# Hybrid mLSTM/attention block on one core: two weight tiles split in an earlier stage, five buffers for the later modulation vectors, one gate on another engine

## The chip, the core and the metric

The kernel runs on one core of a Trainium2 chip. A core has five engines that run side by side and meet at semaphores: TensorE (PE, matrix products and transposes into PSUM), VectorE (DVE), ScalarE (ACT), GpSimd (POOL) and SyncE (SP, which here issues every DMA, in its own order). Each engine works through its instructions strictly in the order in which they stand. The metric is the device time of one execution in microseconds, the median of several runs; lower is better.

## What is computed

One layer over 1024 latent tokens and 256 context tokens, width 1024, float32. The core of it, shortened from the reference:

```python
mod_x = silu(c) @ w_ada + b_ada                       # six vectors of 1024
sh_m, sc_m, gt_m, sh_f, sc_f, gt_f = split(mod_x, 6)
px = modulate(rms_norm(x, g_pre_mix), sh_m, sc_m) @ w_in   # and pc for the context
aq, ak, av, mq, mk, mv, mo, mg = split(px)
att = window_attention(rope(aq), rope(ak), av, kc, vc, sink)
h   = mlstm_bidir(silu(conv(mq)), silu(conv(mk)), mv, mg)   # forward and backward
ml  = rms_norm(h) * gain * sigmoid(mo)
x   = x + gt_m * rms_norm(concat(att, ml) @ w_out, g_post_mix)
f   = swiglu(modulate(rms_norm(x, g_pre_ffn), sh_f, sc_f))
x   = x + gt_f * rms_norm(f, g_post_ffn)
```

## The kernel before

**Products.** Each float32 operand of the large products is split into two fp32r parts, high and low (`split`, lines 58-61: a cast on ACT writes the high part, a subtraction on DVE the low one), and a product is three matmuls: high times high, high times low, low times high.

**Stages up to the attention**, with their times in the profiled execution:

1. to about 40 us: the modulation vectors of the mixing layer (`w_ada`, sections 0 and 1), and the transposed, modulated tokens `hh`, `hl`, `ch`, `cl`.
2. about 40 to 126 us, the V stage: token tiles times the weight slabs for the values and gates (`s1`, `s2`). In its second half `gates()` works out the mLSTM gates, and `ml_weights(n)`, for the eight token blocks n, loads rows of the gates (`w<-a_d`, 512 KB per block), adds and masks them on DVE (L489, eight instructions), exponentiates on ACT (L490), and stores the block to `w_dr` (L491). The blocks n = 0 to 7 lie in the buffers 6, 7, 8, 15, 12, 6, 7, 8 of the shared pool `R`.
3. about 126 to 305 us, the transposed projections: 13 tiles of 128 columns, in the order of `TILES` (mk0, mk1, ak, mq0, mq1, aq0 to aq3, mo0 to mo3). `tload(j)` loads tile j's weights into `tw` (buffer 13 + j % 2) and splits them into `th` (9 + j % 2) and `tl` (11 + j % 2); `tproj(j)` multiplies (L545, L546 with `th`, L548 with `tl`), for the first three tiles with the context's columns (`tc`) as a third output. Then `conv` or `rope` or a sigmoid takes the result from PSUM. Tile j + 1 is loaded while tile j is multiplied.
4. Beside the projections three more sections of `w_ada` are summed on DVE: `ada_rest(sec, j)` streams eight blocks `wb` of 512 KB through two buffers and does `acc += wb * silu(c)` (L596); section 4 after tile ak, section 3 after mq1, section 2 after aq1. `ada_rest2(sec)` reduces `acc` over the partitions on PE (L612 and, for section 2, L606). State steps of the mLSTM (`pk` L643, `mkc` L645, `pu` L649) run between the tiles.

From about 305 us on come the attention with the mLSTM outputs, the output projection (from about 467 us) and the SwiGLU layer.

**What sets the order.** Up to the attention's end, the order on each engine is not that of the code: a scheduler builds it from an own model of durations, under the data's dependencies. A buffer's next user waits for the last user of the same buffer. `issue_after` keeps a DMA behind another on SP; the `wb` blocks of a section stand behind the load of a named tile.

**Transition to the attention.** The last tile, mo3, goes through a sigmoid on ACT (L723) and is scaled by the gain on DVE (L724), then stored. The first attention item's scores (PE L881), their masked copy with a running minimum (DVE L883), exponentials (ACT L892), reciprocal (DVE L894) and normalisation (POOL L897) follow.

## Time and profile before

| | us |
|---|---|
| median of three runs | 1220.74 |
| the three runs | 1224.12, 1219.05, 1220.74 |
| the profiled execution: time | 1219.35 |
| the profiled execution: first to last instruction (span) | 1217.6 |
| PE busy in the span | 1178.2 (97%) |
| DVE, ACT, POOL busy | 819.3, 573.7, 153.4 |
| granted TensorE clock | 0.998 |

The profile names an instruction by its line, engine, operation and tiles; in a row of the timeline the first two numbers are its start and its duration in us, and what stands in brackets is how long the engine had stood idle before it and what ended the idle time. In the view of the waits, a row is: engine and waiting instruction, what released it, total us, times, longest. "SPq" is SP's queue, whose instructions issue DMAs; the time to landing is counted from the issue.

### The profile page before, as it was taken

To read this page: it belongs to the slowest core of one execution; us is meant where nothing else is said; L and a number is where in the kernel's file an instruction comes from. 1 tells how busy PE (TensorE), PEld (TensorE's weight loads), DVE (VectorE), ACT (ScalarE), POOL (GpSimd) and SP (SyncE) were. 2 spreads that over 40 slices of the span, in tenths; PEclk is the share of its full clock that TensorE was granted. 3 is DMA by queue.
4 is the path that set the end of the run, shared out by engine and by line. 5 is a ranking of instruction groups with operands and counts; after the bars stand their busy time and mean duration, and the time that the engine had idled before them with its cause. 6 is when DMAs were issued, how large, how long until landed. Compare 5 with 4: busy or idle time off the path is not lost.

```text
span 1217.6 us, 16271 instructions
## 1 busy us (share of the span) xinstructions
PE 1178.2 (97%) x5859; PEld 963.1 (79%) x5859; DVE 819.3 (67%) x1437; ACT 573.7 (47%) x1066; POOL 153.4 (13%) x196
## 2 busy tenths in 40 slices
PE   6899999999999999999999999999999999999997
PEld 1699788768778777787778888888888888888886
DVE  4873767782888796457867677767867656554566
ACT  5553424121767695777633333333334325434443
POOL 1550001224433382000000000000000000000000
PEclk9999999999999999999999999999999999999999
DMA  9521964767844411421134466466644647665853
GB/s 354 178 70 42 320 201 122 220 176 194 243 128 127 147 49 35 173 89 67 59 106 165 149 217 217 187 233 211 221 154 150 213 149 260 207 217 185 305 191 122
DMA packets 100008, 208.59 MB, mean 171 GB/s; under 512 B 9684, under 2 KB 38740, under 8 KB 98520
## 3 DMA queue, kind: packets, MB, share of 16 engines
q1 hardware_dynamic: 99928, 207.56, 51.5%
q8 instruction: 46, 0.75, 0.3%
q14 instruction: 34, 0.28, 0.1%
HBM read 154.04 MB, written 52.83 MB: 170 GB/s over the span
## 4 chain that ended last, share of the span: by engine, by line
PE 83%; DVE 7%; ACT 4%; DMA 3%; issue 2%; SPq 1%; POOL 0%; DVEq 0%; ACTq 0%
PE xv L74 8%; PE xv L72 8%; PE xv L73 8%; PE pt L74 5%; PE pt L72 5%; PE pt L73 5%; PE t L546 3%; PE t L548 3%; PE t L545 3%; PE op L74 2%; PE op L73 2%; PE op L72 2%; PE fx L72 2%; PE fx L74 2%; PE fx L73 2%
## 5 line engine op out<-in xcount | busy, mean ns | idle before, releaser
L61 DVE TENSOR_TENSOR fo<-fr,fo 128x1024 fp32r<-128x1024 f32 x77 | 92.8, 1223 | 71.4 <-ACT fo L60 66.6
L60 ACT CAST fo<-fr 128x1024 fp32r<-128x1024 f32 x77 | 79.6, 1051 | 74.0 <-PE pt L74 33.2
L545 PE MATMUL t<-hh,th 128*128 128x512 f32 x208 | 82.6, 397 | 0.0
L546 PE MATMUL t<-hl,th 128*128 128x512 f32 x208 | 82.2, 395 | 0.0
L1297 ACT CAST wS<-wr 128x512 fp32r<-128x512 f32 x88 | 54.2, 622 | 55.8 <-PE pt L74 37.4
L1299 DVE TENSOR_TENSOR wS<-wr,wS 128x512 fp32r<-128x512 f32 x88 | 60.4, 689 | 20.7 <-ACT wS L1297 20.7
L548 PE MATMUL t<-hh,tl 128*128 128x512 f32 x208 | 65.4, 394 | 3.0 <-DVE tl L61 3.0
L72 PE MATMUL xv<-tT,wS 128*128 128x512 f32 x168 | 66.1, 393 | 0.0
L74 PE MATMUL xv<-tT,wS 128*128 128x512 f32 x168 | 65.7, 391 | 0.0
L73 PE MATMUL xv<-tT,wS 128*128 128x512 f32 x168 | 65.6, 390 | 0.0
L72 PE MATMUL op<-woh,mh 128*128 128x512 f32 x128 | 51.1, 399 | 1.8 <-ACT mh L60 1.8
L74 PE MATMUL op<-woh,ml 128*128 128x512 f32 x128 | 50.4, 394 | 0.9 <-DVE ml L61 0.8
L73 PE MATMUL op<-wol,mh 128*128 128x512 f32 x128 | 50.0, 391 | 0.0
L1049 DVE TENSOR_TENSOR wr<-wr 128x512 f32<-128x512 f32 x66 | 45.5, 690 | 1.4
L545 PEld LDWEIGHTS t<-hh,th 128*128 128x128 f32 x208 | 39.1, 188 | 8.4 <-issue 0.5
L548 PEld LDWEIGHTS t<-hh,tl 128*128 128x128 f32 x208 | 37.4, 188 | 10.4 <-DVE tl L61 3.2
L546 PEld LDWEIGHTS t<-hl,th 128*128 128x128 f32 x208 | 39.1, 188 | 8.0 <-issue 1.2
L1331 ACT ACTIVATE es<-es 128x512 f32<-128x512 f32 x22 | 13.9, 633 | 66.6 <-DVE es L1052 66.6
L881 PE MATMUL s<-k,qh 128*128 128x256 f32 (+1 forms) x128 | 41.0, 330 | 2.4 <-DVE sm L883 2.2
L72 PE MATMUL pt<-fo 128*128 128x512 f32 x110 | 42.9, 390 | 0.0
L74 PE MATMUL pt<-fo 128*128 128x512 f32 x110 | 42.8, 389 | 0.0
L73 PE MATMUL pt<-fo 128*128 128x512 f32 x110 | 42.8, 389 | 0.0
(993 smaller groups left out, 3401.8 us busy)
## 6 DMA issues: line engine op xcount, KB each, us to landing
wr<-in_wfi SPq DMA_DIRECT2D x44, 512.0 KB, 5.4
wb<-in_wada SPq DMA_DIRECT2D x24, 512.0 KB, 4.4
s_d<-a SPq DMA_DIRECT2D x22, 512.0 KB, 6.6
bt<-in_wfo SPq DMA_DIRECT2D x44, 256.0 KB, 3.7
tb_d<-bt SPq DMA_DIRECT2D x11, 1024.0 KB, 3.9
fr<-s_d SPq DMA_DIRECT2D x44, 256.0 KB, 4.2
fr<-tb_d SPq DMA_DIRECT2D x44, 256.0 KB, 4.4
fr<-a_d SPq DMA_DIRECT2D x33, 256.0 KB, 4.5
```

The source lines that it names most:

```text
L60: act.copy(hi, raw)
L61: dve.tensor_tensor(lo, raw, hi.bitcast(F32), SUB)
L72: pe.matmul(ps, a[0], b[0], start=first, stop=False, **kw)
L73: pe.matmul(ps, a[0], b[1], start=False, stop=False, **kw)
L74: pe.matmul(ps, a[1], b[0], start=False, stop=last, **kw)
L545: pe.matmul(o, wh[:, kt], m[0], start=f, stop=False)
L546: pe.matmul(o, wh[:, kt], m[1], start=False, stop=False)
L548: pe.matmul(o, wl[:, kt], m[0], start=False, stop=l)
L881: pe.matmul(o, qh[:, h, :], k2[g][:, kc], start=True, stop=False)
L1049: dve.tensor_tensor(out, a, b, SUB)
L1297: act.copy(w[:, 0], raw)
L1299: dve.tensor_tensor(w[:, 1], raw, w[:, 0].bitcast(F32), SUB)
```

## The change

Three parts.

1. **Tile loads.** `tload` is moved ahead of the loop of the V stage's last products; tiles 0 and 1 are loaded and split there, ahead of `ml_weights`, and the loop over `TILES` starts its loads with tile 2. Block 4 of `ml_weights` moves from buffer 12 (that of tile 1's low part) to buffer 5.
2. **Five buffers.** The blocks `wb` of `ada_rest` go through five buffers of the pool `p2` in place of two.
3. **Last gate.** For mo3 alone the scaling by the gain is done by POOL in place of DVE.

```diff
     def ml_weights(n):
 
-        wt_ = R((6, 7, 8, 15, 12)[n % 5], f"w{n}", (2, 4, P))
+        wt_ = R((6, 7, 8, 15, 5)[n % 5], f"w{n}", (2, 4, P))
...
+    twd, tws = {}, {}
+
+    def tload(j):
+        wh = R(9 + j % 2, f"th{j}", (KT, P), F32R)
+        wl = R(11 + j % 2, f"tl{j}", (KT, P), F32R)
+        with tc.issue_after(xd[NI - 1].ins):
+            twd[j] = load_split(wh, wl, wt[j], R(13 + j % 2, f"tw{j}", (KT, P)))
+        tws[j] = wh, wl
+
     gates()
     for i in range(NFILL, NI):
         s2(i)
+        if i in (NFILL + 1, NFILL + 2):
+            tload(i - NFILL - 1)
         if i > NFILL:
             ml_weights(i - NFILL - 1)
...
             for kt in range(KT):
-                t = T((1, 3)[kt % 2], f"wb{sec}_{kt}")
+                t = T((1, 3, 4, 5, 6)[kt % 5], f"wb{sec}_{kt}")
                 dma(t, wada[kt * P:(kt + 1) * P, sec * D:(sec + 1) * D])
...
-    tload(0)
     for j, name in enumerate(TILES):
-        if j + 1 < len(TILES):
+        if 1 < j + 1 < len(TILES):
             tload(j + 1)
...
-            dve.tensor_scalar(t, t, vec[:, VGML + i:VGML + 1 + i], None, MUL)
+            g_ = vec[:, VGML + i:VGML + 1 + i]
+            if i == 3:
+                pool.tensor_scalar(t, t, g_, 1.0, MUL, MUL)
+            else:
+                dve.tensor_scalar(t, t, g_, None, MUL)
             dma(so_d[i], t)
```

The scheduler's order changes with it. The rows below are instructions in the order in which they stand on one engine, without times.

DVE, from the last blocks of `ml_weights` into the convolution of tile mk0, before. `w_1281` and `w_1295` are blocks 6 and 7, `tl_1340` is the low part of tile 1, `tl_1440` that of tile 2, `ct` the convolution, `acc_1650` the sum of section 4:

```order
L489 SCALAR_TENSOR_TENSOR w_1281<-w_1281,ucol,mB 128x128 x4
L489 SCALAR_TENSOR_TENSOR w_1295<-w_1295,ucol,mF 128x128 x4
L61 TENSOR_TENSOR tl_1340<-tw_1341,th_1339 128x1024
L489 SCALAR_TENSOR_TENSOR w_1295<-w_1295,ucol,mB 128x128 x4
L61 TENSOR_TENSOR tl_1440<-tw_1441,th_1439 128x1024
L564 TENSOR_SCALAR ct<-cr,vec 128x1024
L565 SCALAR_TENSOR_TENSOR ct<-cr,vec,ct 128x1024
L566 SCALAR_TENSOR_TENSOR ct<-cr,vec,ct 128x1024
L596 SCALAR_TENSOR_TENSOR acc_1650<-wb_0_1652,csil,acc_1650 128x1024
```

The same place after the change (`w_1293` and `w_1307` are blocks 6 and 7; later lines have moved, so that L599 was L596 and L567 to L569 were L564 to L566):

```order
L489 SCALAR_TENSOR_TENSOR w_1293<-w_1293,ucol,mB 128x128 x4
L599 SCALAR_TENSOR_TENSOR acc_1650<-wb_0_1652,csil,acc_1650 128x1024
L599 SCALAR_TENSOR_TENSOR acc_1650<-wb_1_1655,csil,acc_1650 128x1024
L61 TENSOR_TENSOR tl_1440<-tw_1441,th_1439 128x1024
L567 TENSOR_SCALAR ct<-cr,vec 128x1024
L489 SCALAR_TENSOR_TENSOR w_1307<-w_1307,ucol,mF 128x128 x4
L489 SCALAR_TENSOR_TENSOR w_1307<-w_1307,ucol,mB 128x128 x4
L568 SCALAR_TENSOR_TENSOR ct<-cr,vec,ct 128x1024
L599 SCALAR_TENSOR_TENSOR acc_1650<-wb_2_1658,csil,acc_1650 128x1024
L569 SCALAR_TENSOR_TENSOR ct<-cr,vec,ct 128x1024
```

Tile 1's low part has left this place (it now stands in the V stage, behind the low part `hl_103` of token tile 7); two sums of section 4 stand ahead of tile 2's low part, and block 7 and a third sum inside the convolution.

SP, the DMA issues from the table `sint` on, before. `w_dr_944` to `w_dr_947` are the stores of blocks 4 to 7, `tw_1541` and `tw_1678` the weights of tiles 3 and 4, `wb_0` and so on the blocks of section 4:

```order
L516 DMA sint<-in_sinc 128x1024
L487 DMA w_1295<-a_d 128x512
L491 DMA w_dr_944<-w_1227 128x1024
L487 DMA w_1295<-a_d 128x512
L491 DMA w_dr_945<-w_1267 128x1024
L491 DMA w_dr_946<-w_1281 128x1024
L65 DMA tw_1541<-in_wt 128x1024
L595 DMA wb_0_1652<-in_wada 128x1024
L595 DMA wb_1_1655<-in_wada 128x1024
L491 DMA w_dr_947<-w_1295 128x1024
L65 DMA tw_1678<-in_wt 128x1024
```

The same place after the change (L528 was L516, L598 was L595):

```order
L528 DMA sint<-in_sinc 128x1024
L598 DMA wb_0_1652<-in_wada 128x1024
L598 DMA wb_1_1655<-in_wada 128x1024
L491 DMA w_dr_944<-w_1239 128x1024
L487 DMA w_1307<-a_d 128x512 x2
L598 DMA wb_2_1658<-in_wada 128x1024
L598 DMA wb_3_1661<-in_wada 128x1024
L598 DMA wb_4_1664<-in_wada 128x1024
L491 DMA w_dr_945<-w_1279 128x1024
L491 DMA w_dr_946<-w_1293 128x1024
```

Tile 3's load has left (it stands in the V stage now, ahead of `a_d`); two blocks of section 4 are issued ahead of block 7's loads and three more ahead of the stores of blocks 5 and 6.

DVE, the sums of section 2 beside the tiles aq1 to aq3, before (`mkc` is the scaled key of a state step, `tl_2214` and `tl_2368` low parts of later tiles, `cs` the state, `aq` and `rb` the rotary step):

```order
L596 SCALAR_TENSOR_TENSOR acc_2068<-wb_3_2080,csil,acc_2068 128x1024
L645 TENSOR_TENSOR mkc<-pk,wkcol 128x256 x2
L61 TENSOR_TENSOR tl_2214<-tw_2215,th_2213 128x1024
...
L596 SCALAR_TENSOR_TENSOR acc_2068<-wb_6_2089,csil,acc_2068 128x1024
L61 TENSOR_TENSOR aq_2174<-aq_2174,aqh_2184 128x1024
L596 SCALAR_TENSOR_TENSOR acc_2068<-wb_7_2092,csil,acc_2068 128x1024
L645 TENSOR_TENSOR mkc<-pk,wkcol 128x256 x2
```

The same place after the change (L599 was L596, L648 was L645, L585 was L582):

```order
L599 SCALAR_TENSOR_TENSOR acc_2068<-wb_4_2083,csil,acc_2068 128x1024
L648 TENSOR_TENSOR mkc<-pk,wkcol 128x256 x2
L61 TENSOR_TENSOR tl_2214<-tw_2215,th_2213 128x1024
...
L599 SCALAR_TENSOR_TENSOR acc_2068<-wb_7_2092,csil,acc_2068 128x1024
L585 TENSOR_TENSOR aq_2174<-aq_2174,rb 128x1024
L61 TENSOR_TENSOR aq_2174<-aq_2174,aqh_2184 128x1024
L648 TENSOR_TENSOR mkc<-pk,wkcol 128x256 x2
```

One more sum stands ahead of the first `mkc`, and the last sum stands ahead of two instructions of the rotary step that it stood behind or between.

More of the change, by code (lines that the diff above doesn't have):

```diff
@@ L521, in T @@
         return q2.tile([P, S], F32, name=name, tag=f"s{i}")
-    twd, tws = {}, {}
-    def tload(j):
-        wh = R(9 + j % 2, f"th{j}", (KT, P), F32R)
-        wl = R(11 + j % 2, f"tl{j}", (KT, P), F32R)
-        with tc.issue_after(xd[NI - 1].ins):
-            twd[j] = load_split(wh, wl, wt[j], R(13 + j % 2, f"tw{j}", (KT, P)))
-        tws[j] = wh, wl
     def tproj(j, with_ctx):
```

## The prediction

> **What bounds the kernel now.** I read the page first:
>
> ```profile
> PE 1178.2 (97%) x5859; PEld 963.1 (79%) x5859; DVE 819.3 (67%) x1437; ACT 573.7 (47%) x1066; POOL 153.4 (13%) x196
> ```
>
> PE is busy for 1178.2 of 1217.6 us. No matmul is removed, so the change can only fill PE's idle time, 39.4 us over the whole program, and only that part of it which lies where the change acts. The second view is therefore PE's waits, between 90 and 310 us, the V stage's second half to the attention's start:
>
> ```profile
> PE t L548 <- DVE tl L61: 3.0, 1, 3.0
> PE s L881 <- DVE sm L883: 1.6, 1, 1.6
> PE pu L649 <- DVE mkc L645: 1.6, 1, 1.6
> PE ar L606 <- PE t L548: 1.0, 1, 1.0
> PE s L796 <- DVE sm L883: 0.3, 1, 0.3
> ```
>
> Five waits, 7.5 us in all: that is the ceiling of the change, 0.6% of the time. Each is now followed to what is late.
>
> **The first wait, 3.02 us.** The timeline of PE and DVE around it, and two pieces of the chain of waits:
>
> ```profile
> 138.57 0.39 PE L545 MATMUL t<-hh,th 128*128 128x512 f32 x1
> ...
> 140.30 0.40 PE L545 MATMUL t<-hh,th 128*128 128x512 f32 x1
> ...
> 144.64 0.73 PE L548 MATMUL t<-hh,tl 128*128 128x512 f32 x2 [3.02 <-DVE tl L61]
> ```
>
> ```profile
> 134.24 9.03 DMA w_dr<-w
> 143.36 1.24 DVE tl L61
> ```
>
> Tile 1 (mk1) begins at 140.30, multiplies with its high part, and at the first product with the low part finds that part unwritten. It is written into buffer 12, where block 4 of `ml_weights` lies until its store has landed (134.24 + 9.03). With block 4 in buffer 5 and the split in the V stage this order is gone, and `tl` of tile 1 stands some 60 us ahead of its use. What hides the split there:
>
> ```profile
> 75.75 0.95 DVE L248 TENSOR_TENSOR hl<-hraw,hh 128x512 fp32r<-128x512 f32 x1 [1.44 <-ACT hh L247]
> ```
>
> The order puts it two small instructions ahead of this row, where DVE stands idle for 1.44 us; it takes 1.24. Without that cover it would delay the low parts of token tile 7 by 1.24 us. The cast on ACT stood in the V stage already, and tile 3's load, freed with it, goes out while the queue is nearly empty. Gain: **3.02 us**, provided that tile 2 is not late in turn (below).
>
> **The middle waits, 1.58 and 0.99 us.** DVE and PE beside the tiles aq1 and aq2:
>
> ```profile
> 237.49 1.28 DVE L596 SCALAR_TENSOR_TENSOR acc<-wb,csil,acc 128x1024 f32<-128x1024 f32 x1 [0.28 <-DMA wb<-in_wada]
> 242.68 1.28 DVE L596 SCALAR_TENSOR_TENSOR acc<-wb,csil,acc 128x1024 f32<-128x1024 f32 x1 [3.91 <-DMA wb<-in_wada]
> ...
> 256.70 1.28 DVE L596 SCALAR_TENSOR_TENSOR acc<-wb,csil,acc 128x1024 f32<-128x1024 f32 x1
> ```
>
> ```profile
> 244.35 1.10 PE L649 MATMUL pu<-V,mkc 128*64 128x129 f32 x16 [1.58 <-DVE mkc L645]
> ...
> 258.08 1.88 PE L606 MATMUL ar<-acc,ones 128*1 128x512 f32 x4 [0.99 <-PE t L548]
> ```
>
> With two buffers a block can be loaded only when the last sum but one is done; DVE waits 3.91 us for one, and `mkc` stands behind that sum. With five buffers the order on SP has blocks 0 to 4 of section 2 issued ahead of the section's first sum. `mkc` gains one more sum ahead of it (1.2 us, start to start) and loses the 3.91: 2.7 us, over the 1.58 that PE waited. I take **1.58** (ends 0 and 1.58). The second wait is put down to PE itself, but L606 starts 0.10 us after the last sum has ended (256.70 + 1.28 = 257.98), so the sum is what was late. In the new order L606 stands nineteen matmuls earlier, about 4.4 us at 0.23, and PE arrives another 1.58 us sooner; the last sum must therefore come 0.99 + 4.4 + 1.58 = 7.0 us sooner to hide it. It gains 3.91 + 0.28 of waits and two rotary instructions of 1.14 that now stand behind it: 6.5. That is nearly even, so I take **0.5** (ends 0 and 0.99).
>
> **The last gate.** The transition to the attention on PE, DVE, ACT and POOL:
>
> ```profile
> 305.56 0.28 PE L882 MATMUL s<-k,ql 128*128 128x256 f32 x1
> ```
>
> ```profile
> 306.30 0.94 DVE L724 TENSOR_SCALAR so<-so,vec 128x1024 f32<-128x1024 f32 x1 [4.50 <-ACT so L723]
> 307.16 0.74 DVE L883 CUSTOM_DVE_ANT_0 pr__2722<-s,mask,bcr 128x512 f32<-128x512 f32 x1
> ...
> 310.08 0.16 DVE L894 RECIPROCAL sm<-sm 128x2 f32<-128x2 f32 x1
> ```
>
> ```profile
> 308.00 0.73 ACT L892 ACTIVATE pr__2722<-pr__2722,sm 128x513 f32<-128x513 f32 x1 [0.43 <-POOL pr__2811 L870]
> ...
> 309.33 0.19 ACT L892 ACTIVATION_READ_ACCUMULATOR pr__2722<-pr__2722,sm 128x1 f32 x1
> ```
>
> ```profile
> 307.74 0.18 POOL L870 COPY pr__2811<-bcr 128x4 f32<-128x4 f32 x1
> 310.35 1.37 POOL L897 TENSOR_SCALAR pr__2722<-pr__2722,sm 128x512 f32<-128x512 f32 x2 [2.42 <-DVE sm L894]
> ```
>
> Without the gate DVE's four masked copies begin when the first scores are there, at about 305.9 (305.56 + 0.28), not at 307.16. But the exponentials cannot: the first waits for a POOL copy until 308.00, and the second ends at 309.52. So the reciprocal moves only from 310.08 to about 309.6 and POOL's normalisation from 310.35 to about 309.8. That is 0.55 us at most, if POOL is free. The gate now stands on POOL ahead of it, from 307.9. Its price is not in this trace as such; the nearest rows are POOL's own scaling of the same shape by a column and its slowest instruction of that size:
>
> ```profile
> L198 POOL TENSOR_SCALAR xt<-xt,st x9: 1115/1127/2159, 24.3 to 75.0; 128x1024 f32<-128x1024 f32 x9
> L581 POOL TENSOR_TENSOR rb<-rb,sint x5: 2389/2403/3318, 178.8 to 261.2; 128x1024 f32<-128x1024 f32 x5
> ```
>
> At 1.13 it ends at 309.0 and costs nothing; at 2.16 at 310.1, gain 0.3; at 3.32 at 311.2, a loss of 0.85. L198 is the same form, so I take **0.5**.
>
> ```profile
> L724 DVE TENSOR_SCALAR so<-so,vec x4: 753/753/939, 270.5 to 306.3; 128x1024 f32<-128x1024 f32 x4
> ```
>
> Of the four gates on DVE the last took 0.94 us, the others 0.75; POOL was at its products during the last. [...]
>
> **What the change adds: DMA ahead of the convolution of mk0.** In the new order two blocks of section 4 are issued right behind `sint`, ahead of block 7's loads, and three sums stand in DVE's path to the point where the first context output leaves PSUM (ACT L559). That PSUM buffer is the next but one: tile 2's context product needs it. The rows are the issue of `sint` on SP, its time to landing, ACT behind the convolution, the four windows in which the DMA engines are full (their columns end in clock, DMA share and GB/s), and the durations on DVE:
>
> ```profile
> 131.94 1.26 SPq L516 DMA_DIRECT2D sint<-in_sinc  x1
> ```
>
> ```profile
> DMA to landing us min/median/max: 9.4/9.4/9.4
> ```
>
> ```profile
> 150.18 1.06 ACT L567 ACTIVATE mk<-ct 128x1024 f32<-128x1024 f32 x1 [2.54 <-DVE ct L566]
> 151.15 0.35 ACT L559 COPY cr<-tc 128x256 f32<-128x256 f32 x1
> ```
>
> ```profile
> 120.00:125.00 5.00, 5.00 (x31) 5.00 (x30) 4.24 (x17) 2.72 (x5) 0.48 (x3) 1.00 0.97 261
> 125.00:130.00 5.00, 5.00 (x28) 4.49 (x28) 5.00 (x20) 3.10 (x6) 0.54 (x1) 1.00 1.04 410
> 130.00:135.00 5.00, 5.00 (x28) 4.22 (x27) 2.31 (x9) 1.26 (x2) 0.00 (x0) 1.00 0.98 268
> 135.00:140.00 5.00, 5.00 (x28) 4.26 (x27) 3.33 (x12) 2.44 (x4) 0.00 (x0) 1.00 1.00 374
> ```
>
> ```profile
> L489 DVE SCALAR_TENSOR_TENSOR w<-w,ucol,mF 128x128 f32<-128x128 f32 x32 | 9.2, 346 | 6.4 <-issue 3.2 <-DMA w<-a_d 3.2
> ```
>
> ```profile
> 163.84 1.28 DVE L565 SCALAR_TENSOR_TENSOR ct<-cr,vec,ct 128x1024 f32<-128x1024 f32 x1
> 165.04 1.28 DVE L596 SCALAR_TENSOR_TENSOR acc<-wb,csil,acc 128x1024 f32<-128x1024 f32 x1
> ```
>
> `sint` needed 9.4 us and landed at 141.3. Behind it now come two blocks, one store and block 7's loads, four times 512 KB = 2.1 MB; at the mean of the four windows, 328 GB/s, 6.4 us, so block 7 is there at 147.7. DVE then needs 2.1 us for block 7's eight instructions (0.35 each, a little less from start to start), and 1.2 each, from start to start, for the second step of the convolution, the third sum and the third step: 153.4. ACT's L567 and L559 end at about 154.8. PE needs the buffer when tile 2 comes to its first context product: 140.30 + 8 steps of 1.73 (140.30 - 138.57) + five matmuls of 0.23 = 155.3. **Half a microsecond of slack.** At 261 GB/s the loads take 8.0 us and PE stalls 1.1; at 410 not at all. I take **-0.4** (ends 0 and -1.1). Behind ACT's late L559 stand the cast of tile 3 and the copies that free tile 1's PSUM; by the same steps the latter end at about 163, against 168 when tile 3 needs them, and are covered.
>
> **The sum**: 3.02 + 1.58 + 0.5 + 0.5 - 0.4 = 5.2 us off the profiled execution's 1219.35, so 1214.15. That execution lies 1.39 under the median of the three runs, 1220.74; on the median's scale the forecast is **1215.5 us**.
>
> **The rivals.**
>
> *All of it.* The new blocks' DMA is quicker than the mean of the windows, L606 is covered, the gate on POOL takes 1.13: 3.02 + 1.58 + 0.99 + 0.55 = 6.1, or 1214.6 at most, with the 0.3 of the fifth wait 1214.3. For it: the 410 and 374 GB/s windows; against: two others at 261 and 268.
>
> *The prefetch does not reach the sums.* Section 2 cannot begin before its accumulator is cleared and the bias row has landed, so the sums could begin as late as now and fill the same slots: the middle 2.1 us are not gained, 5.2 - 2.1 = 3.1, or 1217.6. For it: the sum of the order shift is nearly even for L606. Against: DVE's idle time there is put down to `wb`, not to the bias row.
>
> *The stall moves to tile 2.* The 2.1 MB ahead of block 7 hold DVE, DVE holds ACT's L559, and PE waits for PSUM in place of the low part. This is the case in which the kernel becomes slower: it decides when the stall passes 0.5 + 1.58 + 0.5 + 3.02 = 5.6, so when block 7 lands 6.1 us later than I reckon, in 12.5 us in place of 6.4, which is 168 GB/s. At 131 GB/s, half of the slowest full window, the 2.1 MB take 16.0, the stall is 9.1, and the time 1220.7 + 3.5 = 1224.2. Against it: no window with a share of 0.97 or more shows under 261.
>
> **Chances and range.** The forecast 0.60, all of it 0.15, no prefetch 0.17, slower 0.08. What a measurement of this kernel can tell from no change is about 0.5%, 6.1 us: the border lies at 1214.6, only 0.9 under my forecast, and all of the second case and a quarter of the first lie below it: faster 0.30. Above 1226.8 lies only a part of the last case: slower 0.04. Same 0.66. The forecast's own range, with the ends of its terms, is 1214.2 to 1217.0; the runs before spread over 5 us, so a median can lie 1.5 off. Range 1212.8 to 1219.5.
>
> **What would show it.** In the changed profile the wait of PE for `tl` L61 is gone and tile 2 starts at about 154.2, with no wait, or one under 1.1 us, at its first context product. No sum of section 2 waits over 1 us for `wb`, and `pu` waits for no `mkc`. L606's wait, if any, is under 1 us. POOL's gate takes 1.1 to 2.2 us and ends before 310 less the shift. After that the program is the old one, some 5 us earlier. A wait of PE for ACT L559 above 1.1 us proves the fourth step wrong; a sum that waits for `wb` as long as before, the second; a span shorter by less than 4 us without either, that PE's waits do not add up as I summed them.

## The result, and the profile after

The changed kernel takes **1210.5 us** (median of 1210.43, 1210.32, 1210.57 and 1213.68), against 1222.03 for the kernel before on the same chip (1224.12, 1219.05, 1220.74, 1223.31): a ratio of 0.9919 with a 95% interval of 0.9899 to 0.994, so 9.9 us less (7.3 to 12.3); the two medians lie 11.5 apart. Forecast were 1215.5, range 1212.8 to 1219.5: the direction was right, the gain about twice what I said, and the time lies 2.3 below the range. The profiled execution took 1210.43 us, span 1208.6.

The busy line of the page, after:

```profile
PE 1176.0 (97%) x5859; PEld 962.6 (80%) x5859; DVE 819.2 (68%) x1436; ACT 574.5 (48%) x1066; POOL 155.1 (13%) x197
```

As many matmuls as before, and yet PE is busy for 2.2 us less. Of these, 1.2 lie between the marks `pg` and `s` that are named below; the rest lies ahead of `pg`, where the busy time differs from one execution of a kernel to the next (85.1 and 87.0 in two of the changed kernel). PE's waits between 90 and 310 us, after:

```profile
PE s L887 <- DVE sm L889: 0.5, 1, 0.5
PE s L802 <- DVE sm L889: 0.3, 1, 0.3
PE pt L917 <- POOL pr__2722 L903: 0.3, 1, 0.3
```

The three large waits (`tl` of tile 1, `mkc`, `ar`) are gone, none over 0.5 us took their place, and the attention's first wait fell from 1.6 to 0.5.

Where the time went is read best from four marks on PE, each the first instruction that writes a tile: `pg` (in the V stage, behind the new splits and ahead of their use), `pk` (the first state step, behind tiles 0 to 3), `s` (the attention's first scores) and `po` (its first output product). PE's timeline at them, before and after:

```profile
99.81 0.45 PE L424 MATMUL pg<-cst,g 128*64 128x128 f32 x4
...
182.37 0.49 PE L643 MATMUL pk<-cst,mkc 128*128 128x128 f32 x3
...
305.21 0.28 PE L881 MATMUL s<-k,qh 128*128 128x256 f32 x1
...
315.03 0.45 PE L921 MATMUL po<-th__2826,av 128*128 128x512 f32 x1
```

```profile
99.21 0.45 PE L424 MATMUL pg<-cst,g 128*64 128x128 f32 x4
...
178.49 0.38 PE L646 MATMUL pk<-cst,mkc 128*128 128x128 f32 x2
...
297.84 0.28 PE L887 MATMUL s<-k,qh 128*128 128x256 f32 x1
...
306.68 0.46 PE L927 MATMUL po<-th__2826,av 128*128 128x512 f32 x1
```

| stretch | before | after | gain |
|---|---|---|---|
| `pg` to `pk` (tile 1's wait) | 82.56 | 79.28 | 3.28 |
| `pk` to `s` (the middle) | 122.84 | 119.35 | 3.49 |
| `s` to `po` (last gate) | 9.82 | 8.84 | 0.98 |
| `po` to the end of PE | 895.95 | 895.93 | 0.02 |
| end of PE to the end of the span | 6.59 | 6.03 | 0.56 |
| ahead of `pg` | 99.81 | 99.21 | 0.60 |

The three places of the change give 3.28 + 3.49 + 0.98 = **7.75 us**; with the three other stretches the 8.9 by which the two profiled executions differ. Of those three, the one ahead of `pg` says nothing: `pg` starts between 98.8 and 100.9 in the profiled executions, whatever the kernel. Two questions are left: why 7.75 and not 5.2, and why the medians differ by more than that.

### The profile page after: what moved, and what is told of

It is laid out like the page before. It is cut to its first block, busy times and chain, and to the rows that moved or that the text cites. A ratio compares the mean times of both kernels' runs of the same rounds, so it can differ in the third digit from the quotient of the medians.

```text
span 1208.6 us, 16267 instructions
## 1 busy us (share of the span) xinstructions
PE 1176.0 (97%) x5859; PEld 962.6 (80%) x5859; DVE 819.2 (68%) x1436; ACT 574.5 (48%) x1066; POOL 155.1 (13%) x197
## 4 chain that ended last, share of the span: by engine, by line
PE 87%; DVE 6%; ACT 5%; issue 1%; DMA 1%; POOL 0%; SPq 0%; DVEq 0%; ACTq 0%
PE xv L74 8%; PE xv L72 8%; PE xv L73 8%; PE pt L74 6%; PE pt L73 6%; PE pt L72 6%; PE t L551 4%; PE t L549 4%; PE t L548 4%; PE op L74 2%; PE op L73 2%; PE op L72 2%; PE slab L73 2%; PE fx L72 2%; PE fx L74 2%; PE fx L73 2%
## 5 line engine op out<-in xcount | busy, mean ns | idle before, releaser
L1305 DVE TENSOR_TENSOR wS<-wr,wS 128x512 fp32r<-128x512 f32 x88 | 60.4, 689 | 20.7 <-ACT wS L1303 20.7
```

Source lines behind the costliest of these rows:

```text
L1305: dve.tensor_tensor(w[:, 1], raw, w[:, 0].bitcast(F32), SUB)
```

## The experiments

In the table below stand the same stretches for every execution that was profiled, taken from PE's rows in the same way; the times were measured beside the kernel before on the same chip (its medians in the four groups of runs: 1219.51, 1221.28, 1221.65, 1219.95).

| kernel | time | ratio to before (95%) | `pg` to `pk` | `pk` to `s` | `s` to `po` | after PE |
|---|---|---|---|---|---|---|
| before | | | 82.56 | 122.84 | 9.82 | 6.59 |
| changed | 1210.50 | 0.9919 (0.9899 to 0.994) | 79.28 | 119.35 | 8.84 | 6.03 |
| 1: tile loads | 1216.15 | 0.9973 (0.9961 to 0.9985) | 79.30 | 122.85 | 9.66 | 6.58 |
| 2: five buffers | 1216.37 | 0.9969 (0.9956 to 0.9982) | 83.18 | 119.35 | 9.64 | 6.03 |
| 3: gate on POOL | 1219.72 | 0.9998 (0.9987 to 1.0009) | 83.20 | 124.28 | 8.85 | 6.55 |
| 4: 1 and 2 | 1211.49 | 0.993 (0.9913 to 0.9946) | 79.28 | 119.35 | 9.63 | 6.03 |
| 5: buffer 5 alone | 1216.80 | 0.9972 (0.9958 to 0.9986) | 79.30 | 123.68 | 10.58 | 6.56 |
| 6: loads, buffer 12 | 1222.68 | 1.0011 (0.9994 to 1.0028) | (moved) | (moved) | 10.54 | 6.33 |
| 7: three buffers | 1214.11 | 0.9947 (0.9929 to 0.9965) | 79.28 | 121.75 | 8.87 | 6.02 |
| 8: merged steps | 1224.94 | 1.0036 (1.0024 to 1.0048) | 79.28 | 132.27 | 8.85 | 6.35 |
| 9: added stalls | 1253.11 | one execution | 79.28 | 150.12 | 10.19 | 6.04 |
| 10: 9 again | 1253.68 | one execution | 79.28 | 147.17 | 10.19 | 6.03 |
| 11: eight in one | 1220.97 | 1.0001 (0.9988 to 1.0015) | 79.28 | 128.51 | 8.84 | 6.04 |
| 12: one by one | 1241.66 | 1.0164 (1.0134 to 1.0193) | 79.28 | 137.80 | 9.49 | 6.03 |
| 13: before again | 1221.88 | one execution | 85.37 | 122.31 | 10.47 | 6.64 |
| 14: before, third | 1218.24 | one execution | 82.29 | 122.85 | 9.64 | 6.61 |
| 15: changed again | 1210.08 | one execution | 79.28 | 119.35 | 8.85 | 6.03 |
| 16: merged, free sums | 1218.19 | 0.9982 (0.9966 to 0.9997) | 79.28 | 125.35 | 8.85 | 6.04 |

Where a stall is gone, its stretch repeats to 0.03 us (79.28 to 79.30, 119.35, 8.84 to 8.87); in 9, 10 and 12, with products added up to the attention, `s` to `po` is longer. Where one stands it can differ between executions of one kernel: 82.29 to 85.37 for `pg` to `pk` in the three of the kernel before.

### The three parts one by one (1 to 4)

Kernel 1 is the change without its other two parts, and so on; against the changed kernel:

```diff
 1, tile loads alone:
-                t = T((1, 3, 4, 5, 6)[kt % 5], f"wb{sec}_{kt}")
+                t = T((1, 3)[kt % 2], f"wb{sec}_{kt}")
 1 and 4, the gate of mo3 back on DVE:
-            if i == 3:
-                pool.tensor_scalar(t, t, g_, 1.0, MUL, MUL)
-            else:
-                dve.tensor_scalar(t, t, g_, None, MUL)
+            dve.tensor_scalar(t, t, g_, None, MUL)
 2 and 3: the kernel before with the one line of part 2, or that of part 3
```

> Part 1 alone: tiles 0 and 1 split in the V stage and block 4 in buffer 5; two buffers for the later modulation vectors, last gate on DVE. Theory A (the gain adds up by place; a break between runs of projection matmuls costs PE busy time as well): the 3.02 us wait for the low part of tile 1 is gone, the pieces pk of the first state steps stand in one run, so PE reaches the first pk 3.2 to 3.3 us sooner and the time is 3.0 to 3.5 us below the kernel before; the waits for mkc (1.6) and for the accumulator (1.0) stay. Theory B (only PE's waits count): -3.0. Rival C (the later gains hang on this part too, because section 4's blocks stand behind tile 3's load): -4.5 or more, with the wait for mkc under 1 us.

> Part 2 alone: five buffers for the later modulation vectors, the rest as before. Theory A: the waits for mkc (1.58) and for the accumulator at the column sums (0.99) are gone, and three breaks between runs of projection matmuls less (two pairs of pu merged, the column sums merged with pk) give about 1.2 us more: -3.4 to -3.9 us. Theory B (only PE's waits): -2.1 to -2.6 us. Rival C (parts hang together): less than -2, with a wait for mkc left. In all of them the 3.0 us wait for the low part of tile 1 stays.

> Part 3 alone: the last gate on POOL, the rest as before. Theory A: POOL's copy for the first attention item still ends near 307.9, since POOL's late products are as late as before, and the exponentials wait for it; so the first output product moves by 0.2 to 0.6 us, time -0.2 to -0.6. Rival (the gate alone makes the whole 0.98 us of the transition): -0.9 to -1.1. Rival (gate behind POOL's products delays the normalisation): 0 to +0.6.

> Parts 1 and 2, the last gate left on DVE as before. Theory A (places add up): -6.8 us, the change without the transition's 0.98; attention starts as early as in the changed kernel, the first output product comes 0.5 to 1.0 us later than there. Rival (the transition's gain comes from POOL's earlier products, which parts 1 and 2 give, not from the gate): -7.3 to -7.8, first output product within 0.3 us of the changed kernel's offset.

By place the parts add up but for 0.2 us of the transition. The tile loads alone make the 3.28 (79.30), the five buffers alone the 3.49 (119.35), and parts 1 and 2 together both of theirs. Rival C, that the parts hang together, is out. In time kernels 1, 2 and 4 are 3.3, 3.8 and 8.5 us below the kernel before; part 3 alone cannot be told from nothing (its interval reaches from -1.6 to +1.1 us). By place the gate alone makes the 0.98 (8.85), the number of the rival; but kernel 4, without the gate, has 9.63 and not 9.82, so 0.19 of the 0.98 came without it. In kernels 2 and 3 the first wait stands, with 2.1 and 2.2 us, and yet `pg` to `pk` is longer than before: something follows the stall there that the profile before does not show (below).

Where the 0.98 comes from: the transition in the changed kernel, on DVE, ACT and POOL,

```profile
298.63 0.75 DVE L889 CUSTOM_DVE_ANT_0 pr__2722<-s,mask,bcr 128x512 f32<-128x512 f32 x1 [6.25 <-PE s L888]
298.91 1.28 ACT L938 ACT_TABLE_LOAD   x1
299.00 1.12 POOL L728 TENSOR_SCALAR so<-so,vec 128x1024 f32<-128x1024 f32 x1 [0.62 <-ACT so L725]
...
299.31 0.74 DVE L889 CUSTOM_DVE_ANT_0 pr__2722<-s,mask,bcr 128x512 f32<-128x512 f32 x1
...
300.21 0.72 ACT L898 ACTIVATE pr__2722<-pr__2722,sm 128x513 f32<-128x513 f32 x1
...
301.76 0.17 DVE L900 RECIPROCAL sm<-sm 128x2 f32<-128x2 f32 x1
```

in kernel 4, with the gate on DVE and POOL done early,

```profile
298.46 0.19 POOL L873 COPY pr__2811<-bcr 128x4 f32<-128x4 f32 x1
...
299.87 0.75 DVE L886 CUSTOM_DVE_ANT_0 pr__2722<-s,mask,bcr 128x512 f32<-128x512 f32 x1
...
300.71 0.73 ACT L895 ACTIVATE pr__2722<-pr__2722,sm 128x513 f32<-128x513 f32 x1 [0.24 <-issue]
```

and in the third execution of the kernel before (14):

```profile
304.59 0.19 POOL L870 COPY pr__2811<-bcr 128x4 f32<-128x4 f32 x1
306.00 0.75 DVE L883 CUSTOM_DVE_ANT_0 pr__2722<-s,mask,bcr 128x512 f32<-128x512 f32 x1
306.85 0.73 ACT L892 ACTIVATE pr__2722<-pr__2722,sm 128x513 f32<-128x513 f32 x1 [0.25 <-DVE sm L883]
```

Counted from `s`, the three things that the first exponential on ACT comes behind (the end of POOL's last copy, of DVE's first masked copy and of ACT's table load), then what follows:

| execution | POOL's copy | DVE's copy | table load | exponential | reciprocal | `po` |
|---|---|---|---|---|---|---|
| before | 2.71 | 2.69 | 2.35 | 2.79 | 4.87 | 9.82 |
| 14: before, third | 0.54 | 2.51 | 2.35 | 2.61 | 4.69 | 9.64 |
| 4: 1 and 2 | 0.54 | 2.51 | 2.36 | 2.60 | 4.69 | 9.63 |
| 3: gate on POOL | 0.88 | 1.55 | 2.36 | 2.38 | 3.93 | 8.85 |
| changed | 0.54 | 1.54 | 2.35 | 2.37 | 3.92 | 8.84 |

With the gate on DVE and POOL early (4 and 14), ACT waits for DVE's first masked copy, which stands behind the gate; without the gate it is held by its own table load, and the reciprocal comes 0.77 sooner. So the gate is worth 0.79 (9.63 less 8.84). In the profiled execution of the kernel before POOL's copies were late, behind products that ended 2.34 after `s`, against 0.04 in the third execution of the same kernel; beside those products the gate on DVE took 0.94 (1.04 in 13, 0.78 in 1, and 0.75 in 2, 4, 5, 6 and 14, where POOL ran nothing beside it), and these 0.19 are the rest of the 0.98. Kernel 3 does not test its theory A: PE came to `s` 2.1 us later there, so POOL was early. No run has the gate moved and POOL as late as in the profile before. The gate took 1.12 us on POOL, and the masked copies beside it 0.74 and 0.75, against 0.75 in kernels 4 and 14, where POOL ran nothing beside them.

### The halves of part 1, and the number of buffers (5 to 7)

```diff
 5, the kernel before with one number changed:
-        wt_ = R((6, 7, 8, 15, 12)[n % 5], f"w{n}", (2, 4, P))
+        wt_ = R((6, 7, 8, 15, 5)[n % 5], f"w{n}", (2, 4, P))
 6, kernel 1 with block 4 back in buffer 12:
-        wt_ = R((6, 7, 8, 15, 5)[n % 5], f"w{n}", (2, 4, P))
+        wt_ = R((6, 7, 8, 15, 12)[n % 5], f"w{n}", (2, 4, P))
 7, the changed kernel with three buffers:
-                t = T((1, 3, 4, 5, 6)[kt % 5], f"wb{sec}_{kt}")
+                t = T((1, 3, 4)[kt % 3], f"wb{sec}_{kt}")
```

> The kernel before with one number changed: block 4 in buffer 5, not 12; the tile loads stay where they were in the code. Theory A (tile 1's low part was late only because its buffer held block 4; with the buffer free the scheduler puts its split early by itself): PE's 3.0 us wait is gone, the first pk comes 3.2 us sooner as with part 1 whole, time -3.0 to -3.5 us. Rival (the move of the loads in the code is what does it): a wait of over 2 us for the low part of tile 1 stays, time within 1 us of before.

> The other half of part 1: the tile loads moved, block 4 still in buffer 12. Theory A (buffer 12 has two users whichever comes first): now block 4 waits until tile 1 is multiplied, and the low part of tile 3, the buffer's next user, waits for block 4's store; PE's wait moves from tile 1 to tile 3, 3 to 6 us long near 170 us, so the time is that of before or up to 3 us longer. Rival (the place of the loads is what matters): no wait above 0.5 us there, time -3.0 to -3.5 us.

> The changed kernel with three buffers for the later modulation vectors in place of five. Theory A (one buffer more than two is enough to load ahead of a sum): the waits for mkc and for the accumulator stay away and the breaks are the same 20, so the time is within 1 us of the changed kernel, 1210 to 1212. Rival (depth counts): one of the waits returns with 0.5 us or more, and the time is 1.5 to 3 us above the changed kernel.

PE's waits between 90 and 312 us in kernels 5, 6 and 7, in this order:

```profile
PE pu L649 <- DVE mkc L645: 1.9, 1, 1.9
```

```profile
PE pk L646 <- ACT cr L562: 1.9, 1, 1.9
PE t L551 <- DVE tl L61: 1.8, 1, 1.8
PE pu L652 <- DVE mkc L648: 1.7, 1, 1.7
```

```profile
PE ar L609 <- issue: 1.2, 1, 1.2
PE pu L652 <- DVE gr L610: 0.9, 1, 0.9
```

Kernel 5: tile 1's wait is gone (79.30) though no load was moved in the code. The buffer was the cause; the scheduler splits tile 1 early by itself as soon as it may. Kernel 6: with the loads moved and buffer 12 kept, block 4 must now wait for tile 1, and the wait goes to tile 3 (`tl`, 1.8 us, at 172 us) and to a state step that got ahead of its place (`pk`, 1.9): not the 3 to 6 us at one place that I had expected, but the same loss, and the time is that of before. Kernel 7: three buffers are not enough. DVE again waits for a block (2.70 us in one piece), the column sums' wait is back, and the middle is 2.4 us longer; the rival, that depth counts, is right.

### What a break costs (8, 11, 12, 16)

Between `pg` and `s` PE's busy time fell by 1.2 us without a matmul less. The order of the changed kernel has 20 groups of other products between projection matmuls in place of 23 (each such group is a break in the run of projection matmuls); two pairs of `pu` groups and one pair of `pk` and `ar` now stand together. PE's timeline around one half of a `pu` pair before, and around the whole after:

```profile
225.96 0.40 PE L546 MATMUL t<-hl,th 128*128 128x512 f32 x1
226.28 0.66 PE L649 MATMUL pu<-V,mkc 128*64 128x129 f32 x8
226.88 0.50 PE L545 MATMUL t<-hh,th 128*128 128x512 f32 x1
227.21 0.39 PE L546 MATMUL t<-hl,th 128*128 128x512 f32 x1
```

```profile
226.12 0.39 PE L549 MATMUL t<-hl,th 128*128 128x512 f32 x1
226.44 1.10 PE L652 MATMUL pu<-V,mkc 128*64 128x129 f32 x16
227.47 0.50 PE L548 MATMUL t<-hh,th 128*128 128x512 f32 x1
227.81 0.40 PE L549 MATMUL t<-hl,th 128*128 128x512 f32 x1
```

From the projection matmul ahead of the group to the second one behind it there would be two ordinary steps, 0.46 us. The half costs 227.21 - 225.96 - 0.46 = 0.79, the whole 1.23, so merging two halves saves 2 x 0.79 - 1.23 = 0.35. Kernels 11 and 12 measure it apart: the same 32 small products, eight at a time or one at a time (`j > 8` are the tiles mo0 to mo3; `pin` keeps the next projection matmul behind them).

```diff
+            pin = j > 8 and kt == 3            # kernel 12: j > 8
+            for _ in range(8 if pin else 0):   # kernel 12: 1
+                tc.keep_in_program_order(pe.matmul(gd, V[:, 0, 0, 0:64], V[:, 1, 0, :], start=True, stop=True))
```

> The changed kernel with 32 small products more (64 by 129, the size of pu), in the tiles mo0 to mo3 eight at a time, after the fourth step of each tile: four breaks more. They cost PE their own time, about 8 x 0.115 + 0.45 = 1.4 us a tile by the merges of pu, 5 to 6 us in all. Nothing of the result depends on them.

> The same 32 products, but one after each of the eight steps of the tiles mo0 to mo3: 22 breaks more between runs of projection matmuls than with eight in one. Theory A (a break costs 0.45 us, as the two merges of pu showed): 9 to 11 us longer than the kernel with eight in one. Rival (a break costs 0.15 us, as the merges of pk with pu showed): 3 to 4 us longer. Theory B (only waits count, breaks cost nothing): the same time within 1 us.

PE's timeline in kernel 11, then in kernel 12:

```profile
262.13 0.39 PE L553 MATMUL t<-hl,th 128*128 128x512 f32 x1
262.45 1.97 PE L558 MATMUL gd<-V 128*64 128x129 f32 x16
...
264.69 0.40 PE L553 MATMUL t<-hl,th 128*128 128x512 f32 x1
```

```profile
261.54 0.39 PE L553 MATMUL t<-hl,th 128*128 128x512 f32 x1
261.86 0.43 PE L558 MATMUL gd<-V 128*64 128x129 f32 x2
...
262.56 0.40 PE L553 MATMUL t<-hl,th 128*128 128x512 f32 x1
```

Eight in one cost 264.69 - 262.13 - 0.46 = 2.10, one alone 0.56: eight breaks cost 8 x 0.56 - 2.10 = 2.4 more than one, **0.34 us for each break more**. No wait stands in these rows; the time is booked as busy. The stage `pk` to `s` is 9.3 us longer in kernel 12 than in 11, of which 22 breaks more are 7.5; the other 1.8 stay open. Of the 20.7 by which the whole kernel is longer (two executions of kernel 12), 10.5 lie in the attention (`po` to the end of PE 906.5 in place of 896.0), where PE waits for ACT's `hs` for 6.4 us in place of 0.6; why is open too. My expectation of 0.45 a break was too high: it left out that the merged place still has its ordinary step of 0.23. Kernel 11 itself missed its expectation: its stage is 9.2 us longer than the changed kernel's, not 5 to 6, for its 16 records take 1.97 us where 16 of `pu` take 1.10.

The same was tried as an improvement. In kernel 8 the state steps are pipelined by one, so that `pk` of step s+1 and `pu` of step s stand in one run; in kernel 16 the column sums are left free.

```diff
...
+            if s_ < 8:
+                for d in range(2):
+                    state_keys(d, s_ + 1)          # pk of the next step
             for d in range(2):
                 state_step(d, s_)                  # now pu alone; it was pk, mkc, pu
+            if s_ < 8:
+                for d in range(2):
+                    state_scale(d, s_ + 1)         # mkc of the next step
```

> The changed kernel with the state steps pipelined by one: the transposes pk of step s+1 and the products pu of step s stand in one run on PE, between two tiles, so 11 breaks in place of 20 between 126 and 298 us; the same number of matmuls. Theory A (each break between runs of projection matmuls costs PE time of its own, 0.2 to 0.48 us by the merges seen): PE reaches the attention 1.8 to 4.3 us sooner than in the changed kernel, time 1206 to 1209, PE busy time lower by as much. Theory B (only PE's waits count, breaks cost nothing): within 0.5 us of the changed kernel. Rival (sums of the modulation vectors, now at fixed places, are late): a new wait at the column sums of over 1 us eats it.

> The merged state steps once more, but with the column sums left to the scheduler, so that they need not wait: 11 breaks in place of 20. By the first merged run the groups pk and pu take 1.79 us together against 0.59 and 1.35 apart, and 0.23 of each gap is the ordinary step from one projection matmul to the next: so next to nothing is left of a gain, 0.1 us a merge, 1 us in all; attention reached within 0 to 1.5 us before the changed kernel, time 1209.5 to 1212. If every break costs 0.35 us as for equal products, 3 us sooner.

The longest wait of PE in kernel 8, then that of kernel 16:

```profile
PE ar L617 <- DVE acc L601: 8.0, 1, 8.0
```

```profile
PE ar L613 <- issue: 3.4, 1, 3.4
```

Both are spoilt by the column sums, which the order now puts ahead of sums that are late; in kernel 16, whose row names no releaser, the last sum ends at 251.01 and the product starts at 251.11. Half clock (next section) comes with both waits: 13.65 us of it (four times 3.41) from 212.7 in kernel 8, 3.41 from 250.8 in kernel 16. Kernel 8 was expected at 1206 to 1209 and kernel 16 at 1209.5 to 1212; both missed by 6 us and more, and in kernel 8 it was the rival with the late sums that came true. The merges themselves brought nothing: a run of `pk` and `pu` takes 1.79 us from one projection matmul to the next, apart they took 0.59 and 1.35, and 0.23 of that is the ordinary step. So 0.34 us is the price of a break between equal products that could stand together, not of every break. No version beats the changed kernel.

### What follows a stall (9, 10, 13 to 15)

Kernels 2 and 3 have a shorter first wait than before and lose more. Busy time of the engines over stretches from the stall on, two in the kernel before and then three in kernel 2 (behind DVE, ACT and POOL stand the granted clock of PE, the DMA share and GB/s):

```profile
139.70:143.11 3.41, 1.92 (x11) 1.46 (x9) 1.06 (x4) 0.39 (x1) 0.00 (x0) 1.00 1.03 415
143.11:146.53 3.42, 1.89 (x10) 1.63 (x11) 3.25 (x7) 3.24 (x6) 0.00 (x0) 1.00 0.40 150
```

```profile
141.38:144.79 3.41, 1.34 (x7) 0.99 (x6) 2.73 (x7) 1.69 (x3) 0.00 (x0) 1.00 0.81 330
144.79:148.21 3.42, 3.42 (x11) 2.79 (x10) 3.38 (x6) 2.66 (x4) 0.00 (x0) 0.50 0.74 246
148.21:151.62 3.41, 3.41 (x20) 2.89 (x19) 2.87 (x3) 1.32 (x2) 0.13 (x2) 1.00 0.98 288
```

In kernel 2 PE is granted half the clock for 3.41 us, makes 11 records of matmuls in place of the 20 of the next stretch, and so loses half of it, 1.71 us; its `pg` to `pk` shows 1.57 (83.18 less 79.28, the wait of 2.07 and the 0.26 that such a wait costs beside its row). In the kernel before it is not, though its stall was longer (3.02 us against 2.07). All drops found in the traces last 3.41 us or a multiple, but for the last one of each, which comes behind PE's end and is cut off by the end of the record; within one execution they begin at whole multiples of 3.41 us from each other (kernel 3: at 41.2, 143.6 and 246.0, 30 times 3.41 apart); that is the rhythm on which I cut the stretches. PE stood idle for 0.61 of the stretch ahead of the drop in kernel 2, and for 0.44 and 0.45 of two stretches in the kernel before: its 3.02 us lay across a boundary. Kernel 9 adds eight stalls (six of them show as waits of PE), and is run twice:

```diff
+            pin = j > 8 and kt in (2, 5)
+            if pin:
...
+                tc.keep_in_program_order(pe.matmul(g1, V[:, 0, 0, 0:64], V[:, 1, 0, :], start=True, stop=True))
...
+                dve.tensor_copy(sc[:, 0:129], g1)
+                for _ in range(n[j, kt]):          # 1 to 5
+                    dve.tensor_scalar(sc, sc, 0.5, None, MUL)
...
+                tc.keep_in_program_order(pe.matmul(g2, sc[:, 0:64], sc[:, 0:129], start=True, stop=True))
```

> The changed kernel with eight added stalls of PE, two in each of the tiles mo0 to mo3: a small product, a copy of it and one to five scalings of a scratch tile on DVE, and a product of that scratch (nothing of the result depends on them). The lengths come to about 1.4, 1.4, 2.2, 2.2, 2.9, 2.9, 3.7 and 4.4 us by the rows of DVE's gates (0.75 us a scaling). Theory A (what the earlier runs showed: a stall can be followed by about 3.4 us at half the granted clock, 1.71 us lost, and whether it is depends on where it falls in a fixed rhythm): the two short ones mostly go without, the ones of 2 to 3 us are hit in part of the cases, the ones of 3.7 and 4.4 us always; two to five such windows in the stage, each of 1.7 us. [...] Theory C (a stall costs its own length and nothing else): no window of half clock at all.

> The same kernel once more, for another position of the rhythm. Theory A: the stalls of 2 to 3 us that are hit differ from the run before, or their number does. [...] If the same ones are hit, the length decides and not the rhythm.

Two of the stalls on PE in the first run, and the same two in the second:

```profile
287.53 0.40 PE L565 MATMUL g<-scr 64*64 64x129 f32 x2 [2.05 <-DVE scr L563]
306.20 0.66 PE L565 MATMUL g<-scr 64*64 64x129 f32 x2 [2.63 <-DVE scr L563]
```

```profile
288.40 0.40 PE L565 MATMUL g<-scr 64*64 64x129 f32 x2 [2.05 <-DVE scr L563]
305.84 0.40 PE L565 MATMUL g<-scr 64*64 64x129 f32 x2 [2.63 <-DVE scr L563]
```

In the first run half clock comes with both, from 288.88 and from 305.95 (the product behind the second stall takes 0.66 in place of 0.40); in the second run, at the same lengths, with neither. Their stretches were idle for 0.60 and 0.70 in the first run, at most 0.35 and 0.46 in the second. The stalls of 1.1 and 1.2 us were never followed by it; with those of 3.35 and 4.07 it stood both times, though in the first run it held already when the 3.35 began. In all seven stretches of the stage were at half clock in the first run and four in the second; I had expected two to five. So length alone does not decide, and theory C is out. Over all profiled executions, from 60 us on up to the stretch in which PE ends, a stretch at full clock was never followed by half clock when PE was idle for less than 0.45 of it, always from 0.50 on, and between the two in some cases (0.45 in the second run of 9 was, 0.46 in the kernel before was not). Ahead of 60 us this does not hold: near 40 us a share of 0.33 was followed by half clock in the first execution of both kernels, and near 25 us one of 0.54 was not in the changed kernel. So the share of idle time in PE's records is not all that counts, and what else does stays open.

> The kernel before, one more profiled execution. Theory A (the clock falls to half for 3.41 us after a stretch of a fixed rhythm in which PE stood idle for about half; the profiled execution before was a lucky one, since its 3.02 us stall was split over two stretches, 0.43 and 0.45 of each): behind the stall of tile 1, the wait for mkc, the first wait of the attention or one of the output projection a window of half clock, one or two of them between 60 and 500 us, each 1.71 us; the execution is longer than the one profiled before by about that. Theory C (the half clock belongs to the experiments, not to the kernel before): none, as in the execution shown.

> The kernel before, a third profiled execution. As for the second: theory A one or two windows of half clock between 60 and 500 us, at one of the same stalls but not always the same; theory C none.

> The changed kernel, a second profiled execution. Theory A: the stalls of tile 1, mkc and the column sums are gone and the attention's first wait is 0.5 us, so no window of half clock between 60 and 320 us, at most one at the waits of 1.2 to 1.5 us ahead of the output projection; its time is then 1210 to 1213. Theory C: none anywhere after 60 us.

| stall | executions in which it stands | followed by half clock |
|---|---|---|
| `tl` of tile 1, 2.1 to 3.3 us | before, 2, 3, 13, 14 | 3 of 5 (2, 3, 13; in 13 twice running) |
| `mkc`, 1.1 to 2.4 us | before, 1, 3, 5, 6, 13, 14 | 3 of 7 (3, 5, 6) |
| attention, gate on DVE, 1.5 to 1.7 us | before, 1, 2, 4, 5, 6, 13, 14 | 3 of 8 (5, 6, 13) |
| attention, gate on POOL, 0.5 us | changed, 3, 7, 8, 11, 12, 15, 16 | 0 of 8 |

The second execution of the kernel before has three such stretches between 60 and 320 us, the third none; the changed kernel none in either. Theory C is out, and theory A has the places right, but not the number: it expected one or two in each execution of the kernel before. The waits ahead of the output projection (1.2 and 1.5 us, from about 440 us on) stand in the changed kernel too; a drop near them stands in kernels 5 and 8 and in the second run of 9, so the changed kernel is not free of the risk.

## Why the prediction was wrong, and where it was right

| term | forecast | measured |
|---|---|---|
| first wait | 3.02 | 3.28 |
| `mkc` | 1.58 | 1.65 |
| column sums | 0.5 (0 to 0.99) | 1.05 |
| last gate | 0.5 (-0.85 to 0.55) | 0.98 |
| tile 2 stalls | -0.4 (-1.1 to 0) | 0 |
| merged groups | not named | 0.7 |
| left over | | 0.1 |
| sum | 5.2 | 7.75 |

The measured waits are what PE's gap between the projection matmuls on both sides lost (before less after); the first is the whole stretch. The sum is that of the two executions shown; with the third execution of the kernel before, which has shorter waits, it is 7.3 (3.01, 3.50 and 0.80).

**The ceiling.** "No matmul is removed, so the change can only fill PE's idle time" is the step that failed first: the five waits made 7.5, of which 0.5 and 0.3 are still there, and the change gained 7.75. A wait costs 0.06 to 0.27 us more than its idle row says (3.28 for 3.02, 1.65 for 1.58, 1.05 for 0.99; in the third execution 3.01 for 2.74), and two merges of `pu` give 0.35 each without any wait. The order of PE showed the merges before the result was known; I had priced only what moved on DVE and SP. The rest of the miss within the sum is in the terms below.

**The first wait**: right in mechanism and place. What hid the split was there, though the split took 2.06 us in its new place and not 1.24; no wait of PE came of it. Tile 2 was not late.

**The middle.** `mkc` as forecast. The column sums were mis-sized. DVE's last sum and PE's products in the changed kernel:

```profile
242.61 2.39 DVE L599 SCALAR_TENSOR_TENSOR acc<-wb,csil,acc 128x1024 f32<-128x1024 f32 x1
```

```profile
246.95 1.88 PE L609 MATMUL ar<-acc,ones 128*1 128x512 f32 x4
```

The sum ends at 245.00 in place of 257.98: 13.0 us sooner, of which the shift at `pk` is 3.9. So it gained 9.1 on its own, not the 6.5 I reckoned, and it is ready 1.95 ahead of the product. Within the section the 6.5 was right: from the start of its first sum to the end of its last it takes 19.46 in place of 26.04, or 6.6 less. What I had not counted is that the first sum starts at 225.54 in place of 231.94, 6.4 sooner, which is 2.5 more than the shift. DVE as a whole waits for the blocks 2.2 us in the changed kernel, in place of 13.2.

**The last gate.** The step "but the exponentials cannot: the first waits for a POOL copy until 308.00" failed. It holds for the execution that I read, where POOL's copy ended 2.71 us after `s` (307.92) and DVE's first masked copy 2.69 (307.90); but I took POOL's lateness as fixed. It belongs to that execution: in the third one of the same kernel POOL's copy ended at 0.54, as in the changed kernel, and DVE alone held ACT. So the exponential came at 2.37, held by the table load, and the transition gained 0.98, of which the gate is 0.79.

**Tile 2.** Block 7 was there by 146.19 and not at 147.7, and PE met no stall. ACT's copy and PE's first context product of tile 2 that needs its buffer:

```profile
152.97 0.35 ACT L562 COPY cr<-tc 128x256 f32<-128x256 f32 x1
```

```profile
154.80 0.28 PE L548 MATMUL tc<-ch,th 128*128 128x256 f32 x1
```

1.5 us of slack in place of the half I had counted; the order of the steps was as I had it, and they cost nothing.

**The median's scale.** The forecast added 1.39 to come from the profiled execution to the median, as if that were a constant. That is the other step that failed, for part of it goes with the stalls: of the 20 stalls of 1.1 to 3.3 us in the table above, 9 were followed by half clock. From the table above the three stalls bring (4/5 + 3/7 + 3/8) x 1.71 = 2.7 us in a mean execution; the second execution of before, with three drops (5.1 us), was 3.1 longer than the first from `pg` on, in part since the wait for `mkc` shrank (1.1 us in place of 1.6), so about 0.6 of that is left, 1.6. With the 7.75 and the 0.56 behind PE, whose cause is open, that is 9.9, the measured gain. This is an estimate from few executions, with the third execution of before it would be 9.5, and that it meets the middle of a wide interval is partly chance; shown is that these drops stand behind the removed stalls and, between 60 and 320 us, in neither execution of the changed kernel.

**The range.** The "own range, with the ends of its terms", 1214.2 to 1217.0, does not follow from those ends: 3.02 + 1.58 + 0.99 + 0.55 and 3.02 - 0.85 - 1.1 off 1220.74 give 1214.6 to 1219.7. Both lie above what was measured.

**The rivals.** "All of it" (6.1) took each term at its upper end, and that was the right direction, but each measured more than its upper end. That the prefetch does not reach the sums, and that the stall moves to tile 2, did not happen. A moved stall did happen in kernel 6, where the buffer was left as it was.

## What to carry to other kernels

Price a stall of the matrix engine not by its idle row alone: add what follows it, and look at several executions, since the same stall of 2.05 us was followed by half clock (3.41 us of it, so up to 1.71 lost) in one execution of kernel 9 and by nothing in the next. When an order changes, count the breaks between runs of matmuls too, for groups of equal products that came together saved time here that no wait shows (0.34 to 0.35 us a merge). And where two releasers end within hundredths of a microsecond of each other, as the copies of POOL and DVE did here (2.71 and 2.69 after `s`), the engine may have to come behind either: with POOL's at 0.54 in the third execution the exponential came only 0.18 sooner. Ask of each whether it will still be there after the change, and look in another execution whether it is always that late.

## What the runs showed that I had not expected

- From 60 us on, half clock for 3.41 us (half of it lost) behind a stretch of 3.41 us in which PE was idle for about half (never under 0.45 of it, always from 0.50 on, in the profiled executions); stalls of 2.05 and 2.63 us were hit in one execution and not in the next.
- DVE's gate of 0.75 us took 0.78 to 1.04 where POOL ran its products and copies beside it.
- 0.34 us for each break more between projection matmuls and equal small products, booked as busy time; nothing where `pk` was merged with `pu` (1.79 us together, 0.59 and 1.35 apart, less the ordinary step of 0.23).
- From the end of PE to the end of the span: 6.02 to 6.04 us in eight of the nine profiled kernels with more than two buffers (6.35 in kernel 8), 6.33 to 6.64 in those with two. The instructions of the engines there are the same; why it differs stays open.
